# Stream kept by token in the second block, the norm applied where products leave PSUM

## The chip, the cores and the metric

One core of a Trainium2 chip runs one launch of the whole program. Times are device microseconds of one launch. A change is told from no change by the median of several launches of each kernel; rows of the trace come from one profiled launch.

## What is computed

256 tokens of width 1024 go through a first block (two mixers, each followed by a mixture of experts) and a second block of four mixers: `nsa` (attention by compressed, selected and sliding keys), `diff` (differential attention), `dilated` and `stick` (stick-breaking attention). Only the second block is changed. Each of its layers is, with its own weights,

```python
def rms_norm(x, gain):
    xf = x.astype(jnp.float32)
    y = xf * lax.rsqrt(jnp.mean(xf * xf, axis=-1, keepdims=True) + EPS)
    return (y * gain.astype(jnp.float32)).astype(x.dtype)

u = rms_norm(h, norm_pre_2[i])
y = mixer(u)          # q, k, v and a gate from u @ w_in; heads; silu(gate) * o @ w_out
h = h + rms_norm(y, norm_post_2[i])
```

In float32 throughout. The mean in `rms_norm` runs over the 1024 channels of a token.

## The kernel before, in words

A product of two float32 operands is made of three products of operands that are split into a high and a low part (`wh`, `wl` of a weight; `uh`, `ul` of the normed stream; `oh`, `ol` of the heads' output): high by low, low by high, high by high. A matmul is 128 rows of contraction, 128 stationary columns and 256 moving ones. A weight chunk of 256 columns comes by one DMA, is cast by ACT (`wh`, L248) and subtracted by DVE (`wl`, L249), and feeds 48 such products.

The stream `xT` lies by channel: 128 channels in the partitions, eight slices of 256 tokens. A layer of the second block goes like this. `pre` (L317) turns the mean square of the stream into a row of reciprocal roots (Ln L285, Exp L286, the row in every partition), and from it a column by token (L327, L329); it builds the normed operand `u` (L334, DVE), `uh` (L335, ACT) and `ul` (L336, DVE and POOL in turn). The first products of a layer, the 192 of `values` (L568), do not wait for that: they take the un-normed `rawh` and `rawl` (gain times stream, L307 and L308), and the column of roots is applied where they leave PSUM. All other products (q, k and the gates) take `uh` and `ul`. Then come the heads, `gate_split` (L599: four chunks, silu of the gate times the output, split into `oh` and `ol`), and `out_proj` (L339): the output by channel, its square (L356) and its product with the gain (L357) from PSUM, the mean square by ones-products (L394), a row of roots again, and slice by slice `y*r` (L411, DVE), the addition to `xT` (L413 DVE, L415 POOL) and `raw_split` for the next layer (L303: L307 ACT, L308 DVE, the square L312, POOL's sum L313, a ones-product L314). The last mixer, `stick`, has an output of its own, `out_last` (L2164), by token; for it the stream is transposed beside the heads (L742, 16 transposes).

In `nsa` the heads are eight score groups (four chunks of q, two groups each). A group has 24 score products (L436, `KH`, `KL`), DVE's masked copy and row maximum (L928), ACT's exponentials (L930), 12 transposes of them (L465), ACT's copies (L467), 8 products with the values (L475), and a normalisation with four transposes (L959).

The order of the instructions on each engine is fixed when the program is built, by a scheduler that takes from each layer's program what it holds ready; some places are tied by hand (`issue_after`). Engines work through their own rows in order.

## Time and profile before

| what | us |
|---|---|
| median of three runs | 1581.42 (1576.27 to 1582.22) |
| profiled execution, its own time | 1575.4 |
| its span | 1573.8 |
| first block, in the span | 0 to about 905 |
| `nsa` | about 905 to 1124 |
| `diff` | about 1124 to 1272 |
| `dilated` | about 1272 to 1411 |
| `stick` | about 1411 to 1573.8 |

The page of the profile gives the busy time of each engine; the windows give the same for any stretch, with the granted clock of TensorE; the groups by line give the mean time of an instruction and what ended the idle time before it; the chain of waits follows the work that ended last.

### The profile page before, as it was taken

To read this page: it belongs to the slowest core of one execution; us is meant where nothing else is said; L and a number is where in the kernel's file an instruction comes from. 1 tells how busy PE (TensorE), PEld (TensorE's weight loads), DVE (VectorE), ACT (ScalarE), POOL (GpSimd) and SP (SyncE) were. 2 spreads that over 40 slices of the span, in tenths; PEclk is the share of its full clock that TensorE was granted. 3 is DMA by queue.
4 is the path that set the end of the run, shared out by engine and by line. 5 is a ranking of instruction groups with operands and counts; after the bars stand their busy time and mean duration, and the time that the engine had idled before them with its cause. 6 is when DMAs were issued, how large, how long until landed. Compare 5 with 4: busy or idle time off the path is not lost.

```text
span 1573.8 us, 26604 instructions
## 1 busy us (share of the span) xinstructions
PE 1426.8 (91%) x10361; PEld 1154.0 (73%) x10361; DVE 974.1 (62%) x2043; ACT 809.6 (51%) x1644; POOL 314.5 (20%) x311
## 2 busy tenths in 40 slices
PE   5989987889599898998799999998999989989998
PEld 3767865566477776767466678775899889979997
DVE  4555669863677556875412366553777776768675
ACT  4455454543366544664212344664456755745574
POOL 2000124322211103111000021322321141322242
PEclk8999999999799998999899999995999999999999
DMA  8700259874699987315799937330354454344520
GB/s 266 236 27 3 94 189 291 260 255 149 212 331 341 348 269 266 106 41 185 245 332 366 344 102 219 107 107 1 113 161 134 135 172 150 129 129 153 160 82 27
DMA packets 243689, 284.71 MB, mean 181 GB/s; under 512 B 14546, under 2 KB 227554, under 8 KB 243556
## 3 DMA queue, kind: packets, MB, share of 16 engines
q1 hardware_dynamic: 236644, 259.85, 50.9%
q0 software_dynamic: 6912, 23.07, 4.5%
q8 instruction: 85, 1.39, 0.4%
q14 instruction: 48, 0.39, 0.1%
HBM read 275.56 MB, written 9.44 MB: 181 GB/s over the span
## 4 chain that ended last, share of the span: by engine, by line
PE 43%; ACT 4%; DVE 2%; POOL 1%; issue 1%; another core or an unknown queue 0%; DVEq 0%; ACTq 0%
PE ps_mm L261 6%; PE ps_mm L263 5%; PE ps_mm L262 5%; PE ps_mm L1992 4%; PE ps_mm L350 3%; PE ps_mm L578 2%; PE ps_x L436 2%; PE ps_x L578 2%; PE ps_t L2032 2%; PE ps_o L475 1%; PE ps_t L1975 1%; ACT wh L248 1%; PE ps_x L465 1%; PE ps_s L2037 1%; PE ps_mm L2175 1%
## 5 line engine op out<-in xcount | busy, mean ns | idle before, releaser
L249 DVE TENSOR_TENSOR wl<-w,wh 128x1024 fp32r<-128x1024 f32 x257 | 321.4, 1258 | 147.0 <-ACT wh L248 143.7
L248 ACT CAST wh<-w 128x1024 fp32r<-128x1024 f32 x261 | 270.0, 1042 | 128.2 <-PE ps_mm L263 59.8
L261 PE MATMUL ps_mm<-uh,wl 128*128 128x256 f32 x720 | 209.3, 291 | 0.0
L262 PE MATMUL ps_mm<-ul,wh 128*128 128x256 f32 x720 | 205.5, 285 | 0.0
L263 PE MATMUL ps_mm<-uh,wh 128*128 128x256 f32 x720 | 204.9, 285 | 0.0
L261 PEld LDWEIGHTS ps_mm<-uh,wl 128*128 128x128 f32 x720 | 136.8, 190 | 4.8 <-issue 1.5
L263 PEld LDWEIGHTS ps_mm<-uh,wh 128*128 128x128 f32 x720 | 136.9, 190 | 1.5 <-issue 0.8
L262 PEld LDWEIGHTS ps_mm<-ul,wh 128*128 128x128 f32 x720 | 137.0, 190 | 1.3 <-issue 0.8
L261 PE MATMUL ps_mm<-wh,xl 128*96 128x256 f32 x256 | 75.8, 296 | 3.5 <-DVE xl L427 3.5
L262 PE MATMUL ps_mm<-wl,xt 128*96 128x256 f32 x256 | 74.2, 290 | 0.0
L263 PE MATMUL ps_mm<-wh,xt 128*96 128x256 f32 x256 | 73.1, 286 | 0.0
L1043 PE MATMUL ps_mm<-w,cond 128*32 128x256 f32 x768 | 55.5, 404 | 15.6 <-DVE mod L1050 9.4
L2074 PE MATMUL ps_s<-w,ht 128*96 128x512 f32 x128 | 57.6, 593 | 0.0
L1992 PE MATMUL ps_mm<-w,xt 128*64 128x256 f32 x384 | 51.5, 384 | 0.0
L261 PE MATMUL ps_mm<-hh,wl 128*128 128x512 f32 (+2 forms) x136 | 47.5, 351 | 2.9 <-DVE qn L1087 2.6
L1043 PEld LDWEIGHTS ps_mm<-w,cond 128*32 128x32 f32 x768 | 22.2, 113 | 37.4 <-DVE mod L1050 12.4
L313 POOL TENSOR_TENSOR rawsq<-rawsq 128x256 f32<-128x256 f32 x16 | 13.7, 857 | 176.7 <-ACT rawsq L312 176.6
L350 PE MATMUL ps_mm<-oh,wl 128*128 128x256 f32 x144 | 42.5, 302 | 6.9 <-DVE sz L609 2.9
L261 PEld LDWEIGHTS ps_mm<-wh,xl 128*96 128x96 f32 x256 | 42.7, 167 | 7.7 <-DVE xl L427 4.5
L262 PE MATMUL ps_mm<-hl,wh 128*128 128x512 f32 (+2 forms) x136 | 47.3, 348 | 0.3 <-DVE hl L1068 0.2
L263 PE MATMUL ps_mm<-hh,wh 128*128 128x512 f32 (+2 forms) x136 | 46.8, 344 | 0.0
L1489 POOL TENSOR_TENSOR xk<-d,KD 128x512 f32<-128x512 f32 x27 | 39.8, 1481 | 33.6 <-PE ps_x L1496 13.2
(654 smaller groups left out, 3998.1 us busy)
## 6 DMA issues: line engine op xcount, KB each, us to landing
w<-mod_w SPq DMA_DIRECT2D x48, 1024.0 KB, 7.3
w<-exp_w_up SPq DMA_DIRECT2D x28, 1024.0 KB, 10.6
w<-exp_w_gate SPq DMA_DIRECT2D x27, 1024.0 KB, 11.9
w<-exp_w_down SPq DMA_DIRECT2D x27, 1024.0 KB, 11.3
w<-b_w_in SPq DMA_DIRECT2D x16, 1024.0 KB, 5.6
w<-d_w_in SPq DMA_DIRECT2D x16, 1024.0 KB, 5.4
w<-a_w_in SPq DMA_DIRECT2D x14, 1024.0 KB, 8.3
w<-c_w_in SPq DMA_DIRECT2D x14, 1024.0 KB, 5.0
```

Of the source, the lines that this page charges most:

```text
L248: nc.scalar.copy(hv, raw[:, i:i + c])
L249: (nc.gpsimd if i and pool_too else nc.vector).tensor_sub(lv, raw[:, i:i + c], hv.bitcast(F32))
L261: nc.tensor.matmul(out, sl(k), mh(k), start=k == ks[0], stop=False)
L262: nc.tensor.matmul(out, sh(k), ml(k), start=False, stop=False)
L263: nc.tensor.matmul(out, sh(k), mh(k), start=False, stop=k == ks[-1])
L350: nc.tensor.matmul(p[:, 256 * m:256 * m + 256], w[a][k][:, 128 * m:128 * m + 128], b[:, k], start=k == 0 and m == 0 and j == 0, stop=k == ...
L436: self.nc.tensor.matmul(out, q[a], k[b], start=j == 0, stop=j == 2)
L578: nc.tensor.matmul(ps[i][:, 256 * t:256 * t + 256], x[a][:, k, ts], w[b][k], start=k == 0 and t == 0 and j == 0, stop=k == KT - 1 and t == ...
L1043: nc.tensor.matmul(p[j:j + 32, :256], self.cond[:, k], w[:, k], start=k < 4, stop=k >= 4)
L1489: nc.gpsimd.tensor_mul(xk, d, Ks)
L1992: nc.tensor.matmul(p[64 * a:64 * a + 64, 256 * j:256 * j + 256], xt[:, k, off + 64 * a:off + 64 * a + 64], w[j][a][k], start=k == 0, stop= ...
L2074: nc.tensor.matmul(p, ht[:, f], w[:, f, cs], start=f == 0, stop=f == 1)
```

## The change

The stream of the second block is kept by token (`hrow`, 128 tokens in the partitions, two halves of 1024 channels). `nsa` makes it from `xT` beside its heads (`rows_of`, 16 transposes and four copies, as `stick` did). `out_proj` works by token for all four layers, in the way `out_last` did: operands swapped, one token half after the other, the mean square as a sum along the row by ACT, roots of one column, the stream updated by two instructions for each half. For the next layer the new stream is transposed back in PSUM (four transposes for each half and 512 channels), and the raw high part (ACT) and raw low part (DVE) are both read from there, 128 columns at a time.

The operand `u`, `uh`, `ul` is gone. All products take the raw operand, and the roots are applied where products leave PSUM: `normed` multiplies 128x512 by the row of roots on DVE (`rq` for q holds the row times 0.125), then ACT casts and DVE subtracts from SBUF. In the three later layers the values products go by token half, so that those of half 0 can go before half 1 is ready. In `nsa` the row is made by `norm_first`, ahead of the values products. The gate columns of `nsa` (48 of them) become products of split parts. The post gain comes as a row by one DMA in each layer.

```diff
-    def pre(self, pool, h, gain):
...
-        for k in range(KT):
-            nc.vector.scalar_tensor_tensor(u[:, k], h[:, k], gain[:, k:k + 1], r, op0=ALU.mult, op1=ALU.mult)
-            nc.scalar.copy(uh[:, k], u[:, k])
-            (nc.gpsimd if k % 2 else nc.vector).tensor_sub(ul[:, k], u[:, k], uh[:, k].bitcast(F32))
-        return (uh, ul), u, rc, r
+    def norm_first(self):
...
+        nc.scalar.activation(self.rr, self.raw_ps[:, :S], AF.Ln, bias=self.eps)
+        nc.scalar.activation(self.rr, self.rr, AF.Exp, scale=-0.5)
         p = self.pst()
         for t in range(2):
+            nc.tensor.matmul(p[:, t:t + 1], self.rr[0:1, 128 * t:128 * t + 128], self.ones[0:1, 0:1], start=True, stop=True)
+        nc.vector.tensor_copy(self.rc, p[:, :2])
+        nc.scalar.mul(self.rq, self.rr, 0.125)
+
+    def rows_of(self, h, t, b):
+
+        p = self.pst()
+        for k in range(4):
+            self.nc.tensor.transpose(p[:, 128 * k:128 * k + 128], h[:, 4 * b + k, 128 * t:128 * t + 128], self.ident)
+        self.nc.vector.tensor_copy(self.h[:, t, 512 * b:512 * b + 512], p)
...
+        def add(t, b):
+            cs = slice(512 * b, 512 * b + 512)
+            dst = h if out is None else y
+            nc.vector.scalar_tensor_tensor(dst[:, t, cs], y[:, t, cs], r[:, t:t + 1], h[:, t, cs], op0=ALU.mult, op1=ALU.add)
...
+            p = self.pst()
+            for k in range(4):
+                nc.tensor.transpose(p[:, 128 * k:128 * k + 128], h[:, t, 512 * b + 128 * k:512 * b + 128 * k + 128], self.ident)
+            for k in range(4):
+                kk = 4 * b + k
+                hi, lo = (x[:, kk, 128 * t:128 * t + 128] for x in self.raw)
+                v, g = p[:, 128 * k:128 * k + 128], ahead[1][:, kk:kk + 1]
+                i = nc.scalar.mul(hi, v, g)
+                j = nc.vector.scalar_tensor_tensor(lo, v, g, hi.bitcast(F32), op0=ALU.mult, op1=ALU.subtract)
+            self.raw_last = i.ins, j.ins
...
+        for t in range(2):
+            product(p, t, 3, w, range(KT))
+            evict(p, t, 3)
+            norm(r[:, t:t + 1], ssq[:, t])
+            for b in range(2):
+                add(t, b)
...
+    def normed(self, wk, p, r, n=2):
+
+        t = wk.tile([128, n, S], F32, name="normed", tag="normed")
+        self.nc.vector.tensor_mul(t, p[:, :n * S].rearrange("p (m n) -> p m n", m=n), r[:, None, :].to_broadcast([128, n, S]))
+        return t
+
+    def split_normed(self, wk, hi, lo, p, r):
+        t = self.normed(wk, p, r)
+        self.nc.scalar.copy(hi, t)
+        self.nc.vector.tensor_sub(lo, t, hi.bitcast(F32))
...
+        order = ([(i, t, k) for t in tiles for i in range(2) for k in range(KT)] if self.by_tile else
+                 [(i, t, k) for k in range(KT) for i in range(2) for t in tiles])
...
-            wg = self.wload(w_in[:, 2560:2608])
+            wg = self.wsplit(w_in[:, 2560:2608])
```

The change also moves instructions, since the scheduler finds other work ready. Three places follow.

TensorE in `nsa`, at the seam of score groups 5 and 6, before. `ps_mm<-uh,wl` is a projection or gate product, `KH,ql` a score, `k_all,e` a transpose of exponentials, `at,vsw` a product with the values, `rb` the normalisation.

```order
L261 MATMUL ps_mm<-uh,wl 128x256
L262 MATMUL ps_mm<-ul,wh 128x256
L263 MATMUL ps_mm<-uh,wh 128x256
L959 MATMUL ps_x<-k_all,rb 128x128 x4
L436 MATMUL ps_x<-KH,ql 128x144 x2
L436 MATMUL ps_x<-KL,qh 128x144 x2
L436 MATMUL ps_x<-KH,qh 128x144 x2
```

And the place where the last projection or gate product stands now: the seam of groups 3 and 4.

```order
L262 MATMUL ps_mm<-rawl,wh 128x256
L263 MATMUL ps_mm<-rawh,wh 128x256
L482 MATMUL ps_x<-k_all,e 128x128 x2
L965 MATMUL ps_x<-k_all,rb 128x128 x4
L453 MATMUL ps_x<-KH,ql 128x144 x2
L453 MATMUL ps_x<-KL,qh 128x144 x2
L453 MATMUL ps_x<-KH,qh 128x144 x2
```

Behind these rows no product with weights follows until the output projection, which starts in group 8 in both kernels. Before, groups 6 and 7 are without one; now groups 4 to 7 are. The products moved: 39 more stand before the first score, and groups 1 to 3 hold 102, 99 and 74, where groups 1 to 5 held 51, 48, 48, 90 and 78.

DVE at the boundary from `nsa` to `diff`, before, from the last evictions of the output (L390) on: `y<-y,rs` is y*r, `rawl` the low part for the next layer.

```order
L390 TENSOR_SCALAR y<-ps_mm,cols_mix 128x256
L390 TENSOR_SCALAR y<-ps_x,cols_mix 128x256
L411 TENSOR_TENSOR y<-y,rs 128x256
L413 TENSOR_TENSOR xT<-xT,y 128x256
L411 TENSOR_TENSOR y<-y,rs 128x256
L308 SCALAR_TENSOR_TENSOR rawl<-xT,cols_mix,rawh 128x256
L411 TENSOR_TENSOR y<-y,rs 128x256
L413 TENSOR_TENSOR xT<-xT,y 128x256
```

Now, from the sum of squares of half 0 on (`rout`, `rc` are the roots of one column):

```order
L359 TENSOR_REDUCE rout<-ssq 128x1
L249 TENSOR_TENSOR wl<-w,wh 128x1024
L366 SCALAR_TENSOR_TENSOR hrow<-y,rout,hrow 128x512 x2
L249 TENSOR_TENSOR wl<-w,wh 128x1024
L378 SCALAR_TENSOR_TENSOR rawl<-ps_x,cols_mix,rawh 128x128
L359 TENSOR_REDUCE rc<-hsq 128x1
L378 SCALAR_TENSOR_TENSOR rawl<-ps_x,cols_mix,rawh 128x128
L356 TENSOR_TENSOR y<-ps_x,gain 128x256
L359 TENSOR_REDUCE rout<-ssq 128x1
L378 SCALAR_TENSOR_TENSOR rawl<-ps_x,cols_mix,rawh 128x128 x3
L366 SCALAR_TENSOR_TENSOR hrow<-y,rout,hrow 128x512 x2
```

The eight steps by channel have become two by token half. Half 0's stream update and its first raw low parts stand ahead of half 1's last eviction (L356).

TensorE in `dilated`, where the last scores of the second pair of heads (`kh`, `ql`) give way to other work, before: gate products follow, 72 of them, then 48 output products.

```order
L436 MATMUL ps_x<-kh,ql 128x256
L436 MATMUL ps_x<-kl,qh 128x256
L436 MATMUL ps_x<-kh,qh 128x256
L261 MATMUL ps_mm<-uh,wl 128x256
L262 MATMUL ps_mm<-ul,wh 128x256
L263 MATMUL ps_mm<-uh,wh 128x256
```

Now output products follow at once:

```order
L453 MATMUL ps_x<-kh,ql 128x256
L453 MATMUL ps_x<-kl,qh 128x256
L453 MATMUL ps_x<-kh,qh 128x256
L710 MATMUL ps_o<-at,v 128x256
L711 MATMUL ps_o<-at,v 128x128
L710 MATMUL ps_o<-at,v 128x256
L711 MATMUL ps_o<-at,v 128x128
L350 MATMUL ps_mm<-wl,oh 128x256 x2
L350 MATMUL ps_mm<-wh,ol 128x256
```

The gate products, 192, stand ahead of these scores now. Between the scores and the point where the second pair's exponentials are needed for the last output products there are 48 output products and then 24 more.

## Rows read from the trace of the kernel before

**Rows 1.** The page, busy us (share of the span) x instructions of each engine.

```profile
PE 1426.8 (91%) x10361; PEld 1154.0 (73%) x10361; DVE 974.1 (62%) x2043; ACT 809.6 (51%) x1644; POOL 314.5 (20%) x311
```

**Rows 2.** Windows: `nsa`, `diff`. Columns: us; busy PE, PEld, DVE, ACT, POOL; clock; DMA; GB/s.

```profile
905.00:1124.00 219.00, 201.11 (x1505) 170.29 (x1504) 125.34 (x347) 116.38 (x281) 53.39 (x61) 0.88 0.34 107
1124.00:1272.00 148.00, 141.59 (x1141) 133.03 (x1140) 109.61 (x227) 95.31 (x199) 32.64 (x27) 1.00 0.45 144
```

**Rows 3.** Windows in `nsa`: filled groups; start of the thin stretch; one group without filler; end.

```profile
995.00:1035.00 40.00, 35.05 (x290) 30.40 (x291) 24.07 (x84) 26.08 (x71) 11.70 (x12) 0.96 0.27 87
1060.00:1065.00 5.00, 4.07 (x24) 2.40 (x21) 2.12 (x12) 1.24 (x6) 0.76 (x1) 0.50 0.44 156
1069.60:1084.40 14.80, 12.74 (x62) 8.41 (x62) 4.47 (x24) 6.02 (x21) 4.94 (x5) 0.50 0.00 0
1095.00:1100.00 5.00, 5.00 (x26) 5.00 (x26) 1.93 (x5) 1.58 (x8) 0.00 (x0) 0.56 0.00 0
```

**Rows 4.** Chain of waits in `nsa`: start us, us, what.

```profile
1037.31 0.44 PE ps_x L959 x4
...
1068.54 1.05 PE ps_x L959 x4
...
1073.42 0.51 ACT e L930 x2
...
1073.97 0.47 PE ps_x L465
...
1104.98 5.80 PE ps_mm L350 x47
```

**Rows 5.** Windows: the three boundaries between layers, and four us in the first output projection.

```profile
1109.00:1113.00 4.00, 3.53 (x30) 3.33 (x30) 2.56 (x3) 2.24 (x5) 0.10 (x1) 1.00 0.34 90
1123.85:1155.30 31.45, 27.49 (x211) 25.66 (x210) 27.16 (x46) 19.60 (x36) 13.82 (x14) 1.00 0.42 131
1272.10:1306.84 34.74, 30.01 (x213) 28.72 (x212) 28.84 (x45) 20.14 (x36) 13.55 (x14) 0.90 0.44 142
1411.16:1443.48 32.32, 28.48 (x212) 27.34 (x212) 27.15 (x45) 19.73 (x36) 11.18 (x12) 0.95 0.45 144
```

**Rows 6.** Chain of waits at the end of `dilated`: start us, us, what.

```profile
1379.16 2.25 DVE lse L682
```

**Rows 7.** Windows: the idle stretch at the end of `dilated`, then full ones in `diff` and `stick`.

```profile
1380.00:1395.00 15.00, 10.55 (x63) 9.38 (x63) 9.49 (x25) 5.13 (x10) 2.66 (x2) 0.89 0.22 70
1150.00:1245.00 95.00, 95.00 (x782) 89.25 (x780) 69.40 (x170) 62.65 (x144) 11.81 (x10) 1.00 0.49 156
1435.00:1560.00 125.00, 125.00 (x1063) 118.88 (x1062) 90.52 (x126) 79.06 (x151) 38.38 (x39) 1.00 0.32 102
```

**Rows 8.** Groups by line and shape, 905 to 1573.8: xcount | busy us, mean ns | idle before, releaser.

```profile
L285 ACT ACTIVATE rs<-ps_x,eps 128x256 f32<-128x256 f32 x6 | 2.8, 472 | 0.8 <-PE ps_x L314 0.8
...
L327 PE MATMUL ps_x<-ones,rs 1*128 1x1 f32 x4 | 0.6, 250 | 1.0 <-ACT rs L286 1.0
...
L850 PE MATMUL ps_mm<-w,u 128*128 128x48 f32 x32 | 3.8, 277 | 0.0
```

**Rows 9.** The same view, instructions of the boundaries and of the output by token.

```profile
L308 DVE SCALAR_TENSOR_TENSOR rawl<-xT,cols_mix,rawh 128x256 fp32r<-128x256 f32 x32 | 18.8, 595 | 4.5 <-ACT rawh L307 4.2
...
L334 DVE SCALAR_TENSOR_TENSOR u<-xT,cols_mix,rs 128x256 f32<-128x256 f32 x32 | 16.9, 596 | 1.6 <-ACT rs L286 1.6
...
L411 DVE TENSOR_TENSOR y<-y,rs 128x256 f32<-128x256 f32 x24 | 13.2, 552 | 4.0 <-ACT rs L286 4.0
...
L357 DVE TENSOR_TENSOR y<-ps_mm,cols_mix 128x512 f32<-128x512 f32 x9 | 6.2, 687 | 5.2 <-ACT ysq L356 5.2
...
L2206 DVE SCALAR_TENSOR_TENSOR y<-y,rout,hrow 128x512 f32<-128x512 f32 x4 | 2.8, 749 | 1.2 <-ACT rout L2203 1.2
...
L390 DVE TENSOR_SCALAR y<-ps_x,cols_mix 128x256 f32<-128x256 f32 x1 | 0.5, 484 | 0.6 <-ACT ysq L389 0.6
...
L2202 ACT ACTIVATE rout<-ssq,eps 128x1 f32<-128x1 f32 x2 | 0.6, 296 | 1.1 <-DVE ssq L2201 1.1
```

More of the change, by code (lines that the diff above doesn't have):

```diff
@@ L391, in out_proj @@
-        if ahead is not None:
-            half = self.split(raw[1][:, :4])
-        for j, k in enumerate((0, 6, 7)):
-            nc.tensor.matmul(ps[:, :S], self.onesD, sq[:, k], start=j == 0, stop=j == 2)
-        r = self.rsqrt(pool, ps[:, :S], S)
-        self.raw = None
-        if ahead is not None:
-            self.raw_begin(ahead[1])
-        last = None
-        def then(f):
-            nonlocal last
-            if last is None:
-                last = f()
-            else:
-                with self.tc.issue_after(last):
-                    last = f()
@@ L409, in out_proj @@
-        for i in range(KT + 2):
-            if i < KT:
-                then(lambda: nc.vector.tensor_mul(y[:, i], y[:, i], r).ins)
-                if i % 2 == 0:
-                    then(lambda: nc.vector.tensor_add(h[:, i], h[:, i], y[:, i]).ins)
-                else:
-                    nc.gpsimd.tensor_add(h[:, i], h[:, i], y[:, i])
-            j = i - LAG
-            if 0 <= j < KT and ahead is not None:
-                then(lambda: self.raw_split(h, j))
-                if j == AT:
-                    with self.tc.issue_after(last):
-                        self.ahead.append([x + y for x, y in zip(half, self.split(raw[1][:, 4:], pool_too=PT))])
+                for t in range(2):
+                    product(p, t, c, ws[c], ks)
@@ new lines, in out_proj @@
+        for t in range(2):
+            for c in range(2):
+                evict(p, t, c)
+        p = [self.pss(), self.pss()]
+        w = weights(2)
+        for t in range(2):
+            product(p, t, 2, w, range(KT))
+            evict(p, t, 2)
+        w = weights(3)
+        if ahead is not None:
+            self.ahead = [self.wsplit(a) for a in ahead[0]]
+            self.raw = [x.tile([128, KT, S], F32R, name=n, tag=n) for x, n in ((self.rawh, "rawh"), (self.ub, "rawl"))]
+            rc = self.hp.tile([128, 2], F32, name="rc", tag="rc")
@@ new lines, in out_proj @@
+        for t in range(2):
+            product(p, t, 3, w, range(KT))
[3 more added lines that the diff above has]
+                add(t, b)
+            if ahead is not None:
+                for b in range(2):
+                    nc.scalar.activation(junk, h[:, t, 512 * b:512 * b + 512], AF.Square, accum_out=hsq[:, t, b:b + 1])
+                norm(rc[:, t:t + 1], hsq[:, t])
+        if ahead is None:
+            return
+        rb = pool.tile([128, 2, 128], F32, name="rb", tag="ysq")
@@ L478, in spread, with diff @@
         self.behind(first, *(i for _, i in ats))
-    def diff(self, h, gpre, gpost, ahead=None):
+    def diff(self, h, gpost, ahead):
         nc, A = self.nc, self.A
@@ L589, in values @@
                     w = self.wsplit(src)
-                for k in range(KT):
-                    product(i, w, k)
+                for t in tiles:
+                    for k in range(KT):
+                        product(i, w, t, k)
             nc.scalar.mul(v[:, 0], ps[i][:, :256], rc[:, 0:1])
@@ L696, in merge, with stick @@
         nc.scalar.copy(o[:, 2 * hd:2 * hd + 2], po.rearrange("p (m n) -> p m n", m=2))
-    def stick(self, h, gpre, gpost, out):
+    def stick(self, h, gpost, out):
         nc, A = self.nc, self.A
@@ L768, in stick_weights, with nsa @@
         return a, nc.scalar.activation(a[:, :384], a[:, :384], AF.Exp).ins
-    def nsa(self, h, gpre, gpost, ahead=None):
+    def nsa(self, h, gpost, ahead):
         nc, A = self.nc, self.A
@@ L799, in nsa @@
                 for m in range(2):
[L800 removed]
+                    self.gemm_cm(p[:, 256 * m:256 * m + 256], w, m, u)
                 pv = p.rearrange("p (m n) -> p m n", m=2)
```

266 lines of the change are left out of this document (100 added, 166 removed).

## Prediction, made before the changed kernel had run

> **What bounds the kernel now.** I read the page first: TensorE (PE) is busy for 91% of the span, no other engine over 62% [rows 1]. Then the windows, one for each of the four layers that the change touches: PE is busy 92% (`nsa`) to 96% (`diff`) there, and VectorE (DVE), next, 57 to 74% [rows 2]; the other two lie between. So in these 669 us a microsecond is won only where PE stands idle, runs at half clock, or gets fewer instructions; shorter work on DVE, ScalarE (ACT) and GpSimd (POOL) pays only where PE waits for it. Then short windows, to find where PE waits. There are three kinds of places. **The tail of `nsa`**: from 1060 to 1100 the granted clock is about half [rows 3]. The chain of waits shows why the stretch stays thin: ACT's exponentials and PE's transposes of them follow each other with no other PE work between [rows 4]. **The three layer boundaries**, from the last output product of a layer to the end of the next layer's 192 values products [rows 5]. **The end of `dilated`**, where PE waits for the merge of its heads [rows 6]. Elsewhere, as from 1150 to 1245 in `diff` and from 1435 to 1560 in `stick`, PE is busy for the whole window [rows 7]. The profiled execution took 1575.4 us, 6.0 below the median of the three runs, so 6.0 goes on at the end.
>
> **The `nsa` tail.** The eight score groups (two for each q chunk) have the same PE work before and after, but the projection products used as filler are handed out otherwise: the order shows groups 6 and 7 without filler before, groups 4 to 7 now; their products stand earlier, 39 of them before the first group. Nothing is saved by that: a 256-column product costs 0.12 us wherever it stands (47 in 5.80 us [rows 4]). A group without filler took 14.80 us, of which PE was busy 12.74 at clock 0.50 [rows 3], so its PE work at full clock is 6.4 us, and in the covered stretch that is all it adds. Two more bare groups: 2 x (14.8 - 6.4) = **+16.8**. The covered stretch gets denser: 995 to 1035 has 40.0 - 35.05 = 4.95 us of PE idle [rows 3], and with 74 to 102 products a group instead of 48 to 90 I let all of it go: **-5.0**. Bounds of the pair: -10 if the clock stays full in the bare groups (see the rivals), +16.8 if no idle is recovered.
>
> The start of `nsa`: the row of reciprocal roots is now made before the 96 values products rather than after 20 of them. PE stands behind Ln and Exp of 128x256, each at most 0.47, and two one-column products of 0.25 [rows 8]: **+1.4** (bound below 0, if the weights come later anyway). Each pair of groups gets four transposes of xT, that were in `stick`: four like them cost 0.44 us at full clock [rows 4] and 1.05 at half [rows 4]. Two sets at each clock: 3.0, less 4 x 0.44 saved in `stick`: **+1.2**. The gate columns go from 32 fp32 products (3.8 us [rows 8]) to 48 in three terms; at no more than 0.12 each that is 5.8, at half of it 2.9: I take 0, bounds -0.9 and +1.9.
>
> **The three boundaries.** Before, they take 31.45, 34.74 and 32.32 us, 98.5 together, with PE idle 4.0, 4.7 and 3.8, and with clocks 1.00, 0.90 and 0.95 [rows 5], which is 0, 3.5 and 1.6 us, 1.7 on average. After: 192 products x 0.12 = 23.0; 16 transposes of the stream and two of the norm, 18 x 0.11 = 2.0; the same mean of 1.7 for the clock; and an idle time. That one hangs on a chain that the trace has only in pieces. Token half 0 leaves PE 24 products (2.9 us) before half 1: the square and y times gain, at most 0.48 each, Ln and Exp of one column, at most 0.30 each, two updates of the stream at 0.75 [rows 9], 0.7 until the transposes land (four are 0.44 [rows 4]), then eight pairs of raw high (ACT) and raw low (DVE). Each half of a pair is half the size of raw low now, so half of 0.60 [rows 9], and two banks can alternate: 0.3 a pair, 2.4 for eight. Sum 6.2; with a reduction, semaphores and weight splits between them I take 8, less the 2.9: PE starts on half 0 some 5 us after its last output product, and its first products need only the first slices, so 4.2 idle; half 1's chain runs beside half 0's 48 products (5.8 us). 23.0 + 2.0 + 1.7 + 4.2 = 30.9, three times 92.7: -5.8. Gone also is a wait for a PSUM buffer between output products, 0.47 us of 4 in the one that the window shows [rows 5], so -1.3 for three. Boundaries **-7.1**. Bounds: -17 (no clock loss, idle 2.2) and +7 (the turns below).
>
> What shows a price for those turns: VectorE's y from PSUM was idle 5.2 us in nine times, released by ACT's square of the same tile [rows 9]; 0.58 each, not much under y's own 0.69 for the same tile. The two readers of one tile go one after the other.
> The Trainium skill (PSUM — Partial Sum Buffer, "PSUM bank collisions raise a hardware error") says that two engines may not access the same bank at the same partitions in the same cycle, so their instructions must be kept apart by waits; the trace agrees (the 0.58). By that rule the new pairs, both read from PSUM where before both read SBUF, are strictly serial in a bank.
> If nothing overlaps, 16 pairs are 16 x 0.60 = 9.6 us instead of 4.8, and a boundary is 4.8 longer; that is a rival below.
>
> **What leaves DVE, ACT and POOL.** Gone from DVE are 32 products u of 0.60 and 24 y*r of 0.55 [rows 9], 32 us, and 28 subtractions and additions of the same size; added are 44 evictions of 128x512 at 0.69 (y's price [rows 9]), 30 us, and some smaller ones. POOL loses 49 operations at its mean of 1.0 (314.5 us in 311 [rows 1]). All of it stood beside PE windows that are full [rows 7], so I cost it at 0 outside the boundaries; the cover is the products queued on PE, and where that runs out (ends of `dilated` and `stick`) I price it there. Each q or k chunk comes 0.69 us later from PSUM through one more DVE step: 0 while the next chunk's 48 products (5.8 us) stand between, as the order has it.
>
> **`dilated` and `stick`.** Before, the second pair of heads has 72 gate and 48 output products as cover, 120 x 0.12 = 14.4 us, and PE is still idle 4.45 in 1380 to 1395 [rows 7]; the chain there is DVE's merge (one step of it takes 2.25 us [rows 6]). Now all 192 gate products stand ahead of the last score blocks, and the cover is 48 + 24: 8.6 us, 5.8 less. DVE comes to the merge with less queued (no u, no ul), which gives some of it back; between 0 and +5.8 I take **+3**. In `stick` the last score group is followed by 24 products where 62 stood: 38 x 0.12 = 4.6 us of cover less; between 0 and 4.6 I take **+2.5**. `diff` has full windows and no change of cover: **0**.
>
> Sum: 16.8 - 5.0 + 1.4 + 1.2 - 7.1 + 3 + 2.5 = **+12.8**. 1575.4 + 12.8 = 1588.2 for such an execution, plus 6.0: **1594** as a median.
>
> **Rivals.** About 0.5%, 7.9 us, can be told from no change, so the borders are 1573.5 and 1589.3.
> (a) *Faster: the boundaries carry it, and the bare groups are shorter.* Boundaries -17; a bare group 11 us, between the 14.8 and its 8.4 at full clock (6.4 and the 2.1 that PE was idle in it [rows 3]), so +9.2 for two; `dilated` and `stick` 0: 9.2 - 5.0 + 1.4 + 1.2 - 17 = -10: 1571. The mechanism at its purest is the clock: if it stays full in groups 4 to 7, two cost 2 x (8.4 - 6.4) = +4.0 and two save 12.8, so the tail gives -8.8 instead of +16.8 and the time is 1568. For it: boundary rows with clock 1.00 [rows 5] although PE idled. Against: the bare groups before held half clock for 40 us with PE busy 86% [rows 3], and the new ones hold the same instructions. It decides for faster once the tail costs under -4 beside -17, or so. Chance 0.22.
> (b) *No change.* The tail costs +12, the boundaries give -11, the ends of `dilated` and `stick` +1: 1584. For it: filler is only moved, and PE's total work is nearly the same. 0.23.
> (c) *Much slower.* The readers of a bank take strict turns: +4.8 at three boundaries on top of the forecast, and the full 5.8 and 4.6 at the two ends: 1594 + 14.4 + 2.8 + 2.1 = 1613. For it: the 0.58 above; against: two banks are filled in turn. 0.12.
> The forecast itself has 0.43; with (c), slower has 0.55.
>
> **Range.** (a) at its purest, 1568, and (c), 1613, are the ends of the priced cases; what lies beyond them (all gains at once, or DVE late everywhere) I put at under 2 in 10: 1568 to 1613. The forecast's own range, from its bounds for the ends of `dilated`, `stick` and the filler's idle time, is 1586 to 1604.
>
> **What would show it.** Windows by layer: `nsa` about 14 us longer with a clock near 0.82 (0.88 before), each boundary 2 us shorter, `diff` as it was. In the tail, PE busy over 80% at 0.50 for some 65 us instead of 40. In the boundary the idle time before the first values product 4 to 5 us, released by DVE's raw low. Wrong would be: bare groups under 11 us or at full clock; boundaries under 28 us or above 33; a new wait of PE for the 128x512 eviction in `diff`, where I price none.

## The result, and the profile after

The changed kernel takes 1596.59 us (median of four, 1595.91 to 1600.52); the kernel before, run beside it, 1578.85 (1572.95 to 1582.22). The ratio is 1.0122, with a 95% interval of 1.0083 to 1.016: slower by 1.2%, 18 us between the medians. The forecast was 1594 and slower. The sum behind it held less well than that: two of its terms were wrong by 7 us or more, in opposite directions.

The profiled launch of the changed kernel took 1600.52 us, the highest of its four, and the one of the kernel before 1575.4, below its median; so the two traces differ by 24.7 us of span where the medians differ by 18. In the first block, whose instructions are the same, the sums of squares before the first values products end at 921.1 against 918.5: 2.6 of the 24.7 are there.

Windows of the changed kernel; the columns are those of [rows 2]. First, of `nsa`, the stretch from the last values product to the first output product, 32 us in score groups 4 to 6, the stretch from group 8's normalisation to the last output product, and the part of it behind the wait that is shown below. Then the three boundaries (last output product to last values product), the end of `dilated`, and windows in `diff` and `stick`.

```profile
936.20:1119.10 182.90, 166.12 (x1174) 133.93 (x1172) 99.57 (x296) 89.68 (x222) 43.76 (x50) 0.80 0.33 103
...
1053.00:1085.00 32.00, 25.76 (x122) 15.80 (x121) 12.62 (x59) 14.49 (x47) 8.63 (x9) 0.50 0.04 14
...
1126.10:1154.40 28.30, 25.50 (x185) 24.12 (x183) 14.02 (x24) 11.90 (x27) 0.00 (x0) 0.88 0.36 112
...
1145.70:1154.40 8.70, 8.68 (x48) 8.51 (x48) 1.06 (x4) 1.92 (x5) 0.00 (x0) 0.64 0.39 123
...
1154.40:1182.70 28.30, 26.14 (x212) 24.96 (x211) 19.42 (x39) 18.79 (x45) 2.31 (x2) 1.00 0.51 153
1302.70:1331.20 28.50, 26.66 (x212) 26.09 (x213) 19.07 (x37) 18.69 (x45) 2.35 (x2) 0.94 0.50 170
1435.70:1464.40 28.70, 26.75 (x213) 26.19 (x213) 19.26 (x37) 18.88 (x46) 0.00 (x0) 0.94 0.47 152
...
1395.00:1410.00 15.00, 12.05 (x74) 10.78 (x73) 9.66 (x42) 11.40 (x36) 7.73 (x7) 0.77 0.22 70
1170.00:1265.00 95.00, 95.00 (x795) 90.26 (x794) 69.53 (x167) 60.97 (x127) 7.87 (x6) 1.00 0.50 156
1445.00:1550.00 105.00, 105.00 (x891) 100.83 (x889) 73.44 (x97) 64.42 (x108) 22.71 (x24) 1.00 0.42 133
```

The same two stretches of `nsa` in the kernel before:

```profile
932.10:1093.80 161.70, 148.03 (x1145) 123.55 (x1143) 89.40 (x282) 88.64 (x227) 41.94 (x50) 0.88 0.37 116
1101.00:1123.85 22.85, 22.38 (x181) 21.17 (x180) 15.12 (x19) 10.33 (x15) 4.78 (x3) 1.00 0.35 106
```

The heads of `nsa` went from 161.7 to 182.9 us. The clock of these rows has two levels, 1.00 and 0.50, so a stretch at a mean of c was at half clock for 2 x (1 - c) of its time; what follows is an estimate that takes PE's work there as twice as long. Before, that is 2 x 0.12 x 161.7 = 39 us at half clock; with PE busy 92% of the stretch some 18 us were lost to it. After, 2 x 0.20 x 182.9 = 73 us and 33 lost. PE's idle time is 13.7 and 16.8. So of the 21.2 us, about 15 are the clock, 3 idle time, and the rest more PE work. The boundaries fell from 98.5 us together [rows 5] to 85.5. The output of `nsa` rose from 22.85 to 28.3. `diff` and `stick` have full windows as before [rows 7].

Groups by line and shape of the changed kernel, 905 us to the end (columns as in [rows 8]): the products of the output's third and last quarters, y from PSUM, the raw pairs and the evictions that multiply by the row of roots.

```profile
L350 PE MATMUL ps_x<-wl,oh 128*128 128x256 f32 x128 | 37.8, 296 | 11.2 <-DVE y L356 11.2
...
L427 DVE TENSOR_TENSOR normed<-ps_mm,rr 128x512 f32<-128x512 f32 x29 | 19.9, 686 | 4.7 <-PE ps_mm L263 4.4
...
L377 ACT ACTIVATE rawh<-ps_x,cols_mix 128x128 fp32r<-128x128 f32 x48 | 17.1, 367 | 1.2
L378 DVE SCALAR_TENSOR_TENSOR rawl<-ps_x,cols_mix,rawh 128x128 fp32r<-128x128 f32 x48 | 16.0, 348 | 2.2 <-ACT rawh L377 0.9
...
L356 DVE TENSOR_TENSOR y<-ps_x,gain 128x256 f32<-128x256 f32 x16 | 6.5, 422 | 16.3 <-ACT ysq L355 16.2
```

PE was idle 11.2 us ahead of products of the output's third and last quarters, always until DVE had read y from PSUM: a new wait in three of the four outputs, and none that the prediction had. Of these, 2.8 us are in the output of `nsa` (the same view from 1136 to 1158 us):

```profile
L350 PE MATMUL ps_x<-wl,oh 128*128 128x256 f32 x30 | 9.9, 331 | 2.8 <-DVE y L356 2.8
```

The chain of waits there shows what PE waited for (start us, us, what):

```profile
1138.47 3.06 PE ps_x L350 x26
...
1141.55 1.06 ACT wh L248
...
1142.64 0.41 DVE wl L249
...
1143.78 0.42 DVE y L356
1144.20 1.13 DVE wl L249
1145.33 0.35 DVE y L356
...
1145.72 7.30 PE ps_x L350 x36
```

The products of the third quarter run on beside the first of these rows, to 1142.9; from there to 1145.72 PE is idle. (The chain's own 4.2 us, from 1141.53, are not all idle time of PE.) The third quarter is in one half of two PSUM banks, and the last quarter goes into the other half of the same banks, so it waits until the third is evicted. The eviction stands behind weight casts (L248) in ACT's order and behind their subtractions (L249) in DVE's; the cast at 1141.55 itself waits for a product that ends at 1141.53. The 48 products behind the wait then ran at a mean clock of 0.64, so the output lost more than the 2.8 us.

### The profile page after: what moved, and what is told of

Read it like the earlier page. It is cut to its first block, busy times and chain, and to the rows that moved or that the text cites. A ratio compares the mean times of both kernels' runs of the same rounds, so it can differ in the third digit from the quotient of the medians.

```text
span 1598.5 us, 26595 instructions
## 1 busy us (share of the span) xinstructions
PE 1441.7 (90%) x10377; PEld 1160.7 (73%) x10377; DVE 960.5 (60%) x2039; ACT 812.1 (51%) x1673; POOL 266.2 (17%) x262
## 4 chain that ended last, share of the span: by engine, by line
PE 42%; DVE 4%; ACT 3%; issue 1%; POOL 1%; another core or an unknown queue 0%; DVEq 0%; ACTq 0%; POOLq 0%
PE ps_mm L261 5%; PE ps_mm L263 5%; PE ps_mm L262 5%; PE ps_mm L1999 4%; PE ps_mm L590 3%; PE ps_x L350 3%; PE ps_x L453 2%; PE ps_x L590 2%; PE ps_mm L350 2%; PE ps_t L2039 2%; PE ps_o L492 1%; PE ps_x L482 1%; DVE wl L249 1%; PE ps_t L1982 1%; PE ps_s L2044 1%
## 5 line engine op out<-in xcount | busy, mean ns | idle before, releaser
L249 DVE TENSOR_TENSOR wl<-w,wh 128x1024 fp32r<-128x1024 f32 x258 | 314.0, 1225 | 179.7 <-ACT wh L248 173.1
L248 ACT CAST wh<-w 128x1024 fp32r<-128x1024 f32 x262 | 270.2, 1040 | 183.7 <-PE ps_mm L263 92.0
L262 PE MATMUL ps_mm<-rawl,wh 128*128 128x256 f32 x720 | 207.0, 287 | 0.0
L261 PE MATMUL ps_mm<-rawh,wl 128*128 128x256 f32 x720 | 206.7, 287 | 0.1
L263 PE MATMUL ps_mm<-rawh,wh 128*128 128x256 f32 x720 | 205.2, 285 | 0.0
L263 PEld LDWEIGHTS ps_mm<-rawh,wh 128*128 128x128 f32 x720 | 137.9, 192 | 2.4 <-issue 1.5
L261 PEld LDWEIGHTS ps_mm<-rawh,wl 128*128 128x128 f32 x720 | 137.1, 190 | 2.3 <-PE ps_x L832 0.4
L262 PEld LDWEIGHTS ps_mm<-rawl,wh 128*128 128x128 f32 x720 | 137.4, 191 | 1.4 <-issue 0.7
L1050 PEld LDWEIGHTS ps_mm<-w,cond 128*32 128x32 f32 x768 | 22.3, 114 | 38.2 <-issue 13.7
L350 PE MATMUL ps_x<-wl,oh 128*128 128x256 f32 x128 | 37.8, 296 | 11.2 <-DVE y L356 11.2
L1496 POOL TENSOR_TENSOR xk<-d,KD 128x512 f32<-128x512 f32 x27 | 39.8, 1482 | 33.5 <-PE ps_x L1503 13.2
L482 PE MATMUL ps_x<-k_all,e 128*128 128x128 f32 x132 | 34.2, 339 | 10.9 <-ACT e L936 10.4
## 6 DMA issues: line engine op xcount, KB each, us to landing
w<-exp_w_gate SPq DMA_DIRECT2D x27, 1024.0 KB, 12.7
w<-a_w_in SPq DMA_DIRECT2D x14, 1024.0 KB, 11.7
```

Source lines behind the costliest of these rows:

```text
L248: nc.scalar.copy(hv, raw[:, i:i + c])
L249: (nc.gpsimd if i and pool_too else nc.vector).tensor_sub(lv, raw[:, i:i + c], hv.bitcast(F32))
L261: nc.tensor.matmul(out, sl(k), mh(k), start=k == ks[0], stop=False)
L262: nc.tensor.matmul(out, sh(k), ml(k), start=False, stop=False)
L263: nc.tensor.matmul(out, sh(k), mh(k), start=False, stop=k == ks[-1])
L350: nc.tensor.matmul(p[t][:, 256 * (c % 2):256 * (c % 2) + 256], o[:, k, 128 * t:128 * t + 128], w[b][k], start=k == 0 and c != 1 and j == 0 ...
```

## The experiments

Group lengths here are read from the trace, from the first score, or from the last of a group's four normalisation transposes, to the last one of the next group. "nsa's heads" is the stretch from the last values product to the first output product. The projection and gate products that stand among the rows of a score group are called its filler; a group without any is bare, one with some is covered. Group lengths and stretches come from one profiled launch each.

| kernel | groups 1 to 8, us | sum |
|---|---|---|
| before | 11.8 12.9 15.5 19.2 16.2 15.5 14.8 17.1 | 122.8 |
| changed | 18.1 22.5 15.8 14.7 16.8 14.9 16.1 17.2 | 136.1 |
| held_filler | 14.7 15.9 18.3 16.6 19.5 15.8 19.0 16.3 | 136.1 |
| two_late | 18.1 20.2 15.1 14.2 15.0 15.0 16.2 17.6 | 131.4 |
| rows_early | 18.1 21.0 14.9 14.7 16.2 15.0 14.8 16.4 | 131.1 |
| direct | 11.8 14.2 18.7 22.8 18.8 15.2 16.1 16.5 | 134.1 |
| idle_products | 18.1 22.5 15.8 13.2 13.4 12.2 14.2 16.4 | 125.8 |
| before_held | 12.1 14.3 11.4 14.7 13.8 15.0 18.3 16.3 | 115.9 |

**Banks of their own (own_banks).**

```diff
+        p = [self.mm(), self.mm()]
         for t in range(2):
             product(p, t, 3, w, range(KT))
```

> The changed kernel, with two PSUM banks of their own for the last quarter of each output projection, instead of the second half of the banks that the third quarter is evicted from. Theory: between the third and the last quarter TensorE waits for the eviction of the third (in the profile of the changed kernel 4.2 us at 1141.5 in nsa, 11.2 us of idle in the whole kernel released by DVE's y); with banks of their own that wait goes, and the time falls by 8 to 14 us, to 1583 to 1589 against 1597. Rival: TensorE waits there for the weights of the last quarter (an ACT cast of 1.06 and DVE subtractions of 1.2 stand in the same stretch); then the time stays within 3 us of 1597.

1589.51 us, 7.1 less; against the kernel before 1.0063 (1.003 to 1.0095). Rows of the groups (the last quarter's products now count under `ps_mm`) and a window from group 8's normalisation to the last output product of `nsa`, in this kernel:

```profile
L350 PE MATMUL ps_x<-wl,oh 128*128 128x256 f32 x64 | 18.1, 282 | 0.0
...
L350 PE MATMUL ps_mm<-wl,oh 128*128 128x256 f32 x192 | 54.5, 295 | 6.2 <-ACT oh L637 5.7 <-DVE y L356 0.3
```

```profile
1127.50:1150.10 22.60, 22.59 (x185) 21.37 (x183) 14.05 (x24) 11.87 (x27) 0.00 (x0) 1.00 0.39 120
```

The 11.2 us are gone (0.3 is left that DVE's y ends), and the output of `nsa` is back at 22.6: the wait was for the eviction, not for weights. The 4.2 us of the expectation are the chain's; PE's idle time in that place was 2.8. In the traces the four outputs are 14 us shorter together (5.8, 3.2, 3.2 and 2.2); the medians give half of that, a little under the 8 to 14 expected. The first boundary is 2.2 longer in this trace, the last values product of `nsa` ends 3.7 later, and the changed kernel's profiled launch was 4 above its median.

**Filler held back (held_filler).**

```diff
-                self.gemm_cm(pz[:, 256 * m:256 * m + 256], w, m, self.raw)
+                with self.tc.issue_after(hold[c]) if hold else ExitStack():
+                    self.gemm_cm(pz[:, 256 * m:256 * m + 256], w, m, self.raw)
...
+                    marks.append(turned)
...
-            self.gate_split(wk, w_in, 2608, o, oh, ol)
+            self.gate_split(wk, w_in, 2608, o, oh, ol, hold=[marks[i] for i in (2, 3, 4, 5)])
```

(`turned` is a group's last normalisation transpose; q chunks 1 to 3 are held in the same way, from the first scores and groups 1 and 2.)

> The changed kernel, with the products of q chunks 1 to 3 and of the four gate chunks of nsa held back: each chunk's 48 products are let go one score group later than the one before, so that groups 1 to 7 have 48 each. Nothing else is changed. Theory: the tail of nsa is long because groups 4 to 7 have no other PE work and run at half clock, 14.7 to 17.2 us each; with 48 products (5.8 us) in each group the clock stays full and a group takes about 13, so first score to last normalisation falls from 136 us by 20 to 28: 1569 to 1577. Rival: a group is held up by its own chain through DVE and ACT whatever PE has beside it; then the earlier groups get longer by what the later ones save, and the time falls by less than 6.

1596.51 us: no gain. My theory failed here in the form in which I had put it. nsa's heads in this kernel, and groups 4 to 7:

```profile
934.80:1113.80 179.00, 157.88 (x1174) 131.88 (x1172) 99.89 (x296) 89.79 (x222) 43.87 (x50) 0.87 0.33 105
1033.00:1103.90 70.90, 62.29 (x439) 50.61 (x437) 35.68 (x129) 39.49 (x107) 21.47 (x20) 0.83 0.19 60
```

The clock did rise, from 0.80 to 0.87, but idle time went from 16.8 to 21.1, and the groups with 48 products took 17 us on average, not 13. The chain in group 4 shows what stands between PE's last product and its next transpose:

```profile
1039.11 1.06 ACT wh L248
...
1040.19 1.22 DVE wl L249
1041.42 0.61 DVE normed L427
...
1042.05 0.63 ACT sz L292
1042.68 0.51 ACT qh L432
1043.19 0.53 ACT sz L293
1043.72 0.49 ACT e L940 x2
1044.21 0.52 ACT sz L294
1044.74 1.37 ACT e L940 x6
```

A weight cast, its subtraction, the eviction and the sigmoid of the filler come first in the queues of ACT and DVE, and the chain spends 7 us there, from the last product at 1039.09 to the next transpose at 1046.15. Filler is not free: 48 products of a gate bring 2 x (1.06 + 1.22) + 0.61 + 0.63 + 0.53 + 0.52 = 6.9 us of ACT and DVE work, and where that stands in front of the group's own, the group is longer. nsa's heads are 3.9 us shorter for four bare groups less, about 1 each.

**Both edits (held_and_banks).**

> Both edits together: own banks for the last quarter of the output projections, and the held filler in nsa. If the two causes are independent, the gains add: 28 to 40 us below 1597, 1557 to 1569, clearly faster than the kernel before (1579). If the wait in the output projection only takes the place of another one, or the filler only shifts the wait to the output of nsa, less than two thirds of the sum of the two single gains.

1586.95 us (ratio to before 1.0063, 1.0037 to 1.0089): 9.6 less, the sum of the two single gains (7.1 and 0.1) within the spread, and not to be told from own_banks alone (1.003 to 1.0095); far from 1557 to 1569, since the held filler gave nothing.

**The values by channel slice (values_by_channel).**

```diff
-            self.by_tile = True
+            self.by_tile = False
```

> The changed kernel, with the values products of the three later layers in the order by channel slice, both token halves of a slice in turn, as before the change, instead of all of half 0 first. Theory: the boundaries got shorter (28.3, 28.5 and 28.7 us against 31.5, 34.7 and 32.3) because half 0's products run while half 1's chain of norm, update and transposes goes on; without that TensorE waits for half 1's first slices, 4 to 6 us at each boundary, and the time rises by 10 to 18: 1607 to 1615. Rival: they got shorter because the chain itself is shorter and DVE and ACT have less beside it; then the order makes less than 4 us.

1614.87 us, 18.3 more. The three boundaries, 32.8, 33.4 and 31.9 us where the changed kernel has 28.3, 28.5 and 28.7:

```profile
1152.60:1185.40 32.80, 29.43 (x211) 28.22 (x211) 19.40 (x39) 18.82 (x45) 2.30 (x2) 0.84 0.43 133
1308.00:1341.40 33.40, 28.78 (x212) 27.63 (x213) 19.19 (x37) 18.71 (x45) 2.34 (x2) 0.90 0.43 144
1447.80:1479.70 31.90, 27.20 (x211) 26.12 (x212) 19.15 (x37) 18.71 (x45) 0.00 (x0) 0.95 0.43 135
```

The sum is 98.1, within 0.4 of the kernel before. In these traces the whole gain of the boundaries is the order by token half; the shorter chain by itself gives none. Of the 12.6 us between 98.1 and 85.5, 6.7 are idle time of PE (12.7 against 6.0), and the clock is lower in the first two windows; the other 6 of the 18.3 lie outside the boundaries.

**The hold on the kernel before (before_held).** The edit of held_filler on its code, where the gates' products read `uh` and `ul`:

```diff
-                self.gemm_cm(pz[:, 256 * m:256 * m + 256], w, m, x)
+                with self.tc.issue_after(hold[c]) if hold else ExitStack():
+                    self.gemm_cm(pz[:, 256 * m:256 * m + 256], w, m, x)
```

> The kernel before the change, with the same hold on the products of q chunks 1 to 3 and of nsa's gate chunks: groups 1 to 7 get 48, 48, 24, 72, 48, 48 and 48 products where the kernel before has 51, 48, 48, 90, 78, 0 and 0. Theory now (a group has a floor of its own in DVE and ACT, and products beside it cost or save little): the groups sum to within 5 us of the 122.8 from first score to last normalisation, and the time stays within 6 us of 1578. Rival (the prediction's price, 8.4 us for each bare group): two groups less without other work, 12 to 17 us gained, 1561 to 1566.

1569.27 us, ratio 0.9966 (0.9936 to 0.9996): the best of all versions, and faster than the kernel before by its interval. The groups sum to 115.9, 6.9 less, and nsa's heads to 151.5, 10.2 less, at a clock of 0.96:

```profile
942.40:1093.90 151.50, 138.56 (x1145) 117.18 (x1144) 91.30 (x282) 88.67 (x227) 43.13 (x50) 0.96 0.40 124
```

That lies between the two theories: covering a bare group saves about 5 us, not 8.4 and not nothing. (The profiled launches differ by only 1.3 us, 1574.15 against 1575.4, because in this trace the last values product of `nsa` ends 10.3 us later; the medians differ by 7.6.)

**Two gate chunks late (two_late).** q is free, and of the gates only the last two are held:

```diff
-            self.gate_split(wk, w_in, 2608, o, oh, ol)
+            self.gate_split(wk, w_in, 2608, o, oh, ol, hold=[None, None, marks[2], marks[3]])
```

> The changed kernel with only the last two gate chunks of nsa held, until the normalisation of groups 3 and 4: the products are 102, 77, 0, 48, 48, 0, 0 in groups 1 to 7, where the changed kernel has 102, 99, 74, 0, 0, 0, 0. Read in the trace, groups 1 to 5 from the first score: 87.9 us in the changed kernel. By the prediction's price (a covered group costs its PE work and about one us more) 77. If a group with 48 products costs about 17, as with the filler held everywhere, 84 or more.

Groups 1 to 5: 82.6 against 87.9, so 5.3 us for one bare group less. Between the two again, nearer to the second; one launch, 1597.99 us.

**The rows of the stream early (rows_early), and with own banks (rows_and_banks).**

```diff
+            for g in range(4):
+                self.rows_of(h, g // 2, g % 2)
             wg = self.wsplit(w_in[:, 2560:2608])
...
-                self.rows_of(h, g // 2, g % 2)
```

> The changed kernel with the 16 transposes of the stream and the four copies in nsa (rows_of) moved from the ends of the four q chunks to a place ahead of the heads, where TensorE has dense products; the filler of the groups is as in the changed kernel (102, 99, 74, then none). Theory: in the bare groups the transposes run at half clock (1.05 us for four) and the copy of 0.69 stands in DVE's queue ahead of the next group's exponentials, 1.5 to 2 us for each chunk, so the time falls by 4 to 7: 1590 to 1593, and groups 5 and 7 come down to the 14.8 of groups 4 and 6. Rival, the price in the prediction, transposes alone: 1 to 2 us, 1595.

1595.94 us, no difference from 1596.59. Groups 5 and 7 came down by 0.6 and 1.3, the groups together by 5.0, but the first score came 3.3 later after the values. The rival was right: only moved.

> The changed kernel with both single edits that should pay: the rows of the stream made ahead of nsa's heads, and own banks for the last quarter of the output projections. If they add: 11 to 16 below 1597, 1581 to 1586, within one per cent of the kernel before (1578). If the gain of the early rows is the transposes alone, 1586 to 1589.

1586.81 us (ratio 1.0068, 1.0042 to 1.0095), what the second case gave.

**Evicted as before (direct, direct_q).** The root is left out of q and the gates in `direct`, of q alone in `direct_q`.

```diff
-                self.qk_chunk(wk, w_in[:, 256 * g:256 * g + 256], qh, ql, self.rq)
+                w = self.wsplit(w_in[:, 256 * g:256 * g + 256])
+                p = self.mm()
+                for m in range(2):
+                    pm = p[:, 256 * m:256 * m + 256]
+                    self.gemm_cm(pm, w, m, u)
+                    self.split_ps(qh[:, m], ql[:, m], pm, 0.125)
...
-            z = self.normed(wk, pz, self.rr).rearrange("p m n -> p (m n)")
+            z = pz if direct else self.normed(wk, pz, self.rr).rearrange("p m n -> p (m n)")
```

> The changed kernel with the products of q and of the gates in nsa evicted as before the change: ACT and DVE split q from PSUM in two halves, the sigmoid reads PSUM, and the root of the norm is left out there. The order then has the filler back nearly as before the change: 25 products ahead of the first score, 51, 48, 68, 100, 48, 0, 0, 0 in the groups (before the change 26, and 51, 48, 48, 90, 78, 0, 0, 0). Theory: it is this eviction that moved the filler, and the moved filler and the eviction's own steps that made nsa longer; from the end of the values to the first output product 162 to 168 us where the changed kernel has 182.9 and the kernel before 161.7, and the time falls by 14 to 20, 1577 to 1583. Rival 1, a bare group costs 5 us more, as the last two runs have it, and nothing else in nsa matters: 8 to 12 less, 171 to 175 and 1585 to 1589. Rival 2, the raw operand, the early norm and the transposes made nsa longer: less than 5.

1595.91 us, and 175.3 for nsa's heads in the trace: 7.6 shorter, just under rival 1's 8 to 12, while the time is outside its 1585 to 1589 and the medians tell no gain. The theory failed. The order says that q's eviction moved the filler; the runs say that having it back is worth little. In this kernel the filler stands nearly as before the change and the same groups are bare, and nsa's heads are still 13.6 us longer than there:

```profile
938.20:1113.50 175.30, 158.22 (x1173) 129.64 (x1171) 96.05 (x292) 88.51 (x226) 41.88 (x50) 0.85 0.34 108
```

By the estimate above some 6 of the 13.6 are the clock, 3.4 idle time and the rest more PE work. Why the clock is lower with the filler back was not tried.

> The same for q alone: q is split from PSUM without the root, the gates go through the 128x512 product with the row of roots as in the changed kernel. The order has 25 products, then 51, 48, 92, 103, 21, 0, 0, 0. If q's eviction sets where the filler stands and the gates' extra step lies beside other work, the stretch from the values to the first output product is within 3 us of the run with both evicted directly; if the gates' four steps of 0.69 stand in DVE's queue ahead of the exponentials, 4 to 8 us longer.

169.4 us (one launch, 1589.56). With the gates' extra step the stretch is shorter by 5.9, not longer, so neither case holds. PE's idle time is 3.2 less (13.9 against 17.1) and some 2 more are the clock, 0.86 against 0.85; the two orders also hand out the filler otherwise, and which of their differences does it is not shown.

**q alone held, with own banks (held_q_and_banks).** The edit of own_banks, and of held_filler the part on q:

```diff
-                self.qk_chunk(wk, w_in[:, 256 * g:256 * g + 256], qh, ql, self.rq)
+                self.qk_chunk(wk, w_in[:, 256 * g:256 * g + 256], qh, ql, self.rq, marks[g - 2] if g > 1 else first_scores if g else None)
```

> The changed kernel, all of it computed, with q chunks 1 to 3 of nsa held back (each let go one score group after the one before) and the gate chunks free behind them, and own banks for the last quarter of the output projections: 4 products ahead of the first score, then 48, 48, 80, 142, 18, 0, 0, 0. Theory: most of the filler's place before the change is back, so from the values to the first output product 168 to 174 us, and with the banks (8 us) the time is 1576 to 1582, the same as the kernel before (1577). If holding q only moves the loss into the filled groups, as holding all of it did, 1586 or more.

1585.65 us (ratio 1.005, 1.003 to 1.0071), nsa's heads 179.9: the loss moved into groups 3 and 4 (20.9 and 22.9), as holding all of it had done. The median is 3.9 below own_banks, which the intervals (1.003 to 1.0095 there) do not tell from none.

**Products that nobody reads (idle_products).** With own banks, in `turn_causal`, with `warm` 10 in groups 4 to 7 and 0 elsewhere:

```diff
         p = self.pst()
+        for i in range(warm):
+            with self.tc.issue_after(self.sc_last):
+                nc.tensor.matmul(p[:, :256], self.raw[0][:, 0, :128], self.raw[0][:, 0], start=i == 0, stop=i == warm - 1)
```

> The changed kernel with own banks (1589.5, its nsa with 14.7 to 16.8 us in groups 4 to 7), and in groups 4 to 7 of nsa 40 products each that nothing reads: ten 128x256 products of the raw operand into the bank that the transposes of the exponentials overwrite next, between a score block and these transposes. They add 4.8 us of TensorE work to each group and none to ACT or DVE; the filler ahead of group 4 stays where it is. Theory: a bare group is long because its clock is half (in nsa of the changed kernel 73 us at half clock between the values and the output cost 31 us, against 39 us and 17 before the change); with the added work the clock stays full, and groups 4 to 7, 62.5 us together, fall to 46 to 54 although they do more: 1573 to 1582. Rival: the chain through DVE and ACT sets a group's length; then 62 or more, and 1589 or more.

1577.79 us, ratio to the kernel before 1.0006 (0.999 to 1.0021): 11.7 less than own_banks with 160 more products. nsa's heads and groups 4 to 7, first in own_banks, then here:

```profile
939.90:1120.50 180.60, 163.54 (x1172) 131.75 (x1171) 99.29 (x296) 89.67 (x222) 43.71 (x50) 0.82 0.33 104
1048.30:1110.80 62.50, 50.22 (x255) 31.01 (x253) 24.57 (x117) 27.75 (x92) 19.51 (x19) 0.57 0.06 18
```

```profile
936.70:1109.30 172.60, 163.66 (x1333) 142.22 (x1331) 98.84 (x296) 89.75 (x222) 44.29 (x50) 0.96 0.35 110
1046.80:1099.80 53.00, 49.21 (x414) 40.17 (x413) 23.81 (x117) 27.95 (x92) 20.09 (x19) 1.00 0.07 21
```

The groups' own work is the same, ACT and DVE are as busy as before, the clock is 1.00 instead of 0.57, and the four groups take 53.0 instead of 62.5. This is the run that settles it: a bare group is long because of its clock. (Of the 11.7 between the medians the traces have 8.0 in nsa's heads; the last values product before them also ends 3.2 earlier.)

## Why the prediction was right, and where its steps were not

- **Two more bare groups, +16.8: right in what it names, open in its size.** The bare groups took 14.7 to 16.8, as the row of before had it (14.80 [rows 3]), and idle_products shows the cause. In the trace of the changed kernel nsa's heads lose some 15 us more to the clock and 3 to idle time. But that is not all the filler's doing: with as many bare groups as the kernel before, `direct` still takes 13.6 more, so handing the filler back is worth 7.6 there and 13.5 in `direct_q`, one trace each, and not 16.8. What failed is the sentence that in a covered group PE's work is all it adds: two_late and before_held put the difference between bare and covered at about 5, held_filler at about 1, since the filler's own casts and evictions stand in ACT's and DVE's queues.
- **The covered stretch, -5.0: too much.** From the first score to the last product with weights, PE's idle time went from 5.1 us (978.2 to 1053.9) to 2.1 (990.0 to 1046.6): 3.0 back. By the prediction's own prices it is less: groups 1 to 3 took 56.4 us for 3 x 6.4 + 275 x 0.12 = 52.2 of PE work, 4.2 lost; groups 1 to 5 before 75.6 for 5 x 6.4 + 315 x 0.12 = 69.8, 5.8 lost. That is 1.6 back.
- **The early norm, +1.4: 1.5.** Rows of the chain of the changed kernel, from the last ones-product to the first values product:

```profile
918.81 2.32 PE ps_t L314 x4
...
921.16 0.48 ACT rr L321
...
921.67 0.42 ACT rr L322
...
922.13 1.01 PE ps_t L325 x4
923.14 0.94 PE ps_mm L590 x3
```

  Ln and Exp as in [rows 8]; the two one-column products took 1.01 for 0.50, because PE was at half clock (0.50 from 921.1 to 923.1). That is 2.0, of which the kernel before had 0.5 as well, among its values products:

```profile
922.43 0.53 PE ps_x L327 x4
```

- **The gate columns, 0: +2.6, above the bound of +1.9.** Windows of the 48 products in the changed kernel and of the 32 before:

```profile
966.80:973.20 6.40, 6.40 (x51) 6.40 (x50) 5.74 (x8) 4.38 (x7) 0.00 (x0) 0.83 1.10 348
```

```profile
962.90:966.70 3.80, 3.80 (x36) 3.80 (x34) 3.26 (x5) 2.81 (x5) 0.00 (x0) 0.94 1.10 349
```

  Up to 970.96 the products of 48 columns start 0.11 us apart, hardly less than the 0.12 of 256 columns; the last of them fall to half clock.
- **The boundaries, -5.8: right in sign, -13.0 in size.** The mis-sized term is the idle time: 2.2, 1.8 and 2.0 us in the three windows, where I had 4.2 in each. The first values product comes 2.8 us after the last output product in all three, not some 5, and the windows lose less to the clock (1.00, 0.94, 0.94 against 1.00, 0.90, 0.95). A raw pair took 0.37 and 0.35, more than the 0.30 that I had from half of a 256-column row; that did not matter, since half 1's pairs ran beside half 0's products. Of the strict turns of rival (c) no price shows: DVE's raw low waited 0.9 us for ACT in all 48, and half 1's eight pairs at the first boundary took 3.6 us (1162.64 to 1166.19), 0.45 a pair, where one after the other would be 0.72; the pairs of two banks overlapped.
- **The wait for a PSUM buffer, -1.3: wrong in sign.** I took away an old wait and did not see the new one, though the code shows it: the last quarter's product shares its banks with the third, and the kernel before has the same code in its last layer, where its trace has the wait:

```profile
L2175 PE MATMUL ps_x<-wl,oh 128*128 128x256 f32 x32 | 9.1, 283 | 1.3 <-DVE y L2181 1.3
```

  From group 8's normalisation on, the output of `nsa` rose by 5.5 us; banks of their own take back 5.8 there, 3.2 each in `diff` and `dilated` and 2.2 in `stick`, in the traces, and 7.1 of the whole by the medians.
- **`dilated`, +3: -3 without the new wait.** From its last values product to its last output product 104.3 before, 104.5 after, and some 3 of that are the new wait (own_banks has 101.2). PE is idle 3.0 of 15 at the end, at a clock of 0.77, where it was 4.45 at 0.89 [rows 7]. The lost cover cost nothing that shows. **`stick`, +2.5 and the transposes' -1.8: +3.5** (124.2 and 127.7), of which own_banks takes back 2.2.
- **The sum.** By stage, from the edges of the windows of both traces (us; a layer's row goes from the end of its boundary to its last output product, that of `stick` to the end; the forecast's terms are put where they belong, -0.4 for each of three outputs):

| stage | before | changed | difference | forecast |
|---|---|---|---|---|
| first block, to the sums of squares | 918.5 | 921.1 | +2.6 | none |
| to nsa's last values product | 13.6 | 15.1 | +1.5 | +1.4 |
| nsa's heads | 161.7 | 182.9 | +21.2 | +14.8 |
| nsa's output | 30.1 | 35.3 | +5.3 | -0.4 |
| three boundaries | 98.5 | 85.5 | -13.0 | -5.8 |
| `diff` | 116.8 | 120.0 | +3.2 | -0.4 |
| `dilated` | 104.3 | 104.5 | +0.2 | +2.6 |
| `stick` | 130.3 | 134.1 | +3.8 | +0.7 |

  Heads, outputs and `stick` came out some 19 us worse than forecast, boundaries and `dilated` some 10 better: the errors to the good paid for about half of the others. By the medians the change costs 17.7 us where the sum has 12.8; half of that miss does not show in the time, because the kernel before ran 2.6 faster beside the changed one than in the three launches that the forecast started from. The direction was right by the tail of `nsa`, which carried it; that the time came within 3 us is luck.
- **Slips in the working.** If the clock stayed full, the tail with the covered stretch would be -8.8 - 5.0 = -13.8, not the -10 given as a bound. Rival (a) has +4.2 for that pair and is still faster at 1571, so its border is near +6, not -4. The forecast's own bounds give 1588.5 to 1604, not 1586. The clock was not half all the way from 1060 to 1100 before: it was 0.89 from 1086 to 1090. None of these changed the forecast.

## What to carry to other kernels

Price a scheduler's new order by what it leaves bare: a group of short products and exponentials that was left alone ran mostly at half clock (0.57) and took 15.6 us (62.5 in four), and 13.3 at full clock with 40 products more that nobody reads. That is not the whole loss in the heads of `nsa`: with the filler nearly back in its old place they stayed 13.6 us longer. Filler that needs casts and evictions is worth less than its TensorE time, since these stand in the queues of the engines on which the chain waits. When an output is evicted in parts, look which parts share a PSUM bank: the next product waits for the last reader of that bank, wherever that reader stands in its own queue.

## What was not expected

In the bare groups of the changed kernel the clock was 0.50 for 32 us without a break (1053 to 1085), with PE busy in 25.76 of them; with 40 further 128x256 products in each group it was 1.00 for the whole stretch, PE busy 49.21 of 53.0. And work added to the bounding engine made the program 11.7 us faster.

The Trainium skill (PSUM — Partial Sum Buffer, "PSUM bank collisions raise a hardware error") says that two engines collide at different addresses of one bank as well, if the partitions are the same, and that such accesses have to be kept apart by semaphores. The trace agrees as far as it goes: the last quarter's product waits for the readers of the other half of its bank, 11.2 us of idle in the changed kernel and 0.3 with banks of their own. Whether the chip needs that wait no run shows, since every kernel has it wherever a bank is shared. Whether it could be shorter with the eviction ahead of the cast in ACT's order was not tried.
